# Rotary angles brought into range in radians, with sixteen VectorE operations for thirty

## The chip, the cores and the metric

The kernel runs on one core of one Trainium2 chip. The metric is device time in microseconds (us) of one execution; lower is better. A core has five engines that run side by side, each through its own queue in a fixed order: TensorE (PE; its weight loads are shown as PEld), VectorE (DVE), ScalarE (ACT), GpSimd (POOL) and SyncE (SP, which here only issues DMAs).

## What is computed

The reference is one layer of a hybrid block over 512 positions of 2048 channels: an RMS norm, one wide input projection, a retention branch (8 heads of 256) and a state-space branch, two branch projections merged by gates, an output projection, and a last norm. All of it is float32. The change touches only the rotation of q and k in the retention branch:

```python
def rope(t, positions):
    half = t.shape[-1] // 2
    inv_freq = ROPE_THETA ** (-jnp.arange(half, dtype=f32) / half)
    ang = positions.astype(f32)[..., None] * inv_freq
    cos, sin = jnp.cos(ang)[:, :, None, :], jnp.sin(ang)[:, :, None, :]
    t1, t2 = t[..., :half], t[..., half:]
    return jnp.concatenate([t1 * cos - t2 * sin, t2 * cos + t1 * sin], axis=-1)
```

Positions go up to about 100,000, so an angle can hold many whole turns. They have to be taken off before the sine is looked up, without losing the float32 product's own digits. The table of angles is 128 frequencies (partitions) by 512 positions, and is needed once: all heads share `sinR` and `cosR`.

## The kernel before, in words

Activations lie with channels on the partitions and the 512 positions along the free axis. Each projection is cut into units of 256 columns (`pair`, `unit`). A float32 operand is split into a high part in the matmul's own format (`whi`, by ScalarE, L152) and the rest (`wlo`, by VectorE, L155), and three products of parts stand for one float32 product (L242 to L244). A unit is either *plain* (four block products) or goes by seven block products for eight (`SEVEN`). The seven need sums of blocks: of the weights (VectorE, L259 to L265, from the buffer `wf` that SP loads at L256) and of the activations. The activations' operand tiles `a0` to `a7` (`first_half`) serve both kinds of unit; `b0` to `b7` (`second_half`) only the seven. `collected` brings a unit's result from the accumulator banks `pb` or `att` into a tile `o` (ScalarE L318 or L327, VectorE L319, L320 or L328 to L331). Only then can the next unit that uses the same banks begin.

The order of work: instructions are written down in program order, and a planner puts them in each engine's queue by priority, by dependences and by its own estimate of the time. Two things tie it down. `InOrder` (the lower-case `pe`, `act`, `dve`) keeps all instructions issued through one object in the order of their writing. `behind(ins, other)` keeps one instruction after another on the same engine. Operations written through either show line L122 in the profile.

The start (L427 to L488): SP loads the eight blocks of x; ScalarE squares them; TensorE sums the squares over the channels with a matrix of ones; VectorE adds the two halves of every second square beforehand (L456) and multiplies dt's weights by the norm weights (L461). Then come the norm's inverse root, the product for dt (L466), and for each block the normalization and `first_half` (L474 to L487). `formed` (L488) is the last ScalarE instruction of these, the cast of `a7`.

The rotary tables are a generator, `rotary_tables` (L386 to L424), that yields after each operation; `step(n)` runs the next n. Its operations use the tiles `Q`, `K` and one half of `S`, which are free at that time, and go through `dve`. One is issued at L446, and AHEAD[i] after block i (L459), 18 in all. Head 0 then computes the units of V and the gate together (`two_plain`, L597), writes the second halves in a loop with `step(4)` after each (L602 to L606), and `step(99)` issues what is left, the two sine activations on ScalarE among it. Next come the units Q (plain) and K (seven) of head 0, each followed by the rotation (L562 to L565), and then the scores. So the remaining rotary operations and the second halves form one ordered chain on VectorE.

The exponential of `a_log` (L497) is written for head 1, but its data are there early; it is bound `behind` `formed`.

Of the kernel before, what the change touches and what calls it, by code (L numbers as in the profile page):

```python
# [8 lines left out]
F32 = mybir.dt.float32  # L9
F32R = mybir.dt.float32r  # L10
I32 = mybir.dt.int32
AF = mybir.ActivationFunctionType
ALU = mybir.AluOpType
# [3 lines left out]
P = 128  # L17
# [16 lines left out]
C_ID, C_TRI, C_ONE, C_FREQ, C_END = 0, 128, 256, 384, 386  # L34


def _parts_of_inverse_two_pi():

    digits = 0.15915494309189533576888376337251436203445964574045644874766734405889
    from fractions import Fraction  # L40


    def atan_inv(n, bits):
        one = 1 << bits
        term = one // n
        total, k, sign = term, 1, 1
        while term:
            term //= n * n
            k += 2
            sign = -sign  # L50
            total += sign * (term // k)
        return total

    bits = 240
    pi = 4 * (4 * atan_inv(5, bits) - atan_inv(239, bits))
    inv = Fraction(1 << bits, 2 * pi)
    assert abs(float(inv) - digits) < 1e-15
    parts = []
    for i in range(5):
        step = Fraction(1, 1 << (14 + 12 * i))  # L60
        n = inv // step
        parts.append(float(n * step))
        inv -= n * step
    return parts


def constants():
# [37 lines left out]
PLAIN_Q, PLAIN_K = (0,), ()  # L105
PLAIN_B, PLAIN_X, PLAIN_Z, PLAIN_M = (), (), (), (15,)
PRIO = 30
AHEAD = (2, 1, 3, 1, 3, 1, 3, 3)
ROOT = 4
TERMS = ((0, 0), (0, 1), (1, 0))  # L110
BLOCK = (0, 4, 8, 7)
# [20 lines left out]
def hybrid_block(tc, A, out):  # L132
    nc = tc.nc
    PE, ACT, DVE, POOL, SP = nc.tensor, nc.scalar, nc.vector, nc.gpsimd, nc.sync
# [3 lines left out]
    cst = ctx.enter_context(tc.tile_pool(name="cst", bufs=1))  # L138
    hp = ctx.enter_context(tc.tile_pool(name="hp", bufs=1))
    wp = ctx.enter_context(tc.tile_pool(name="wp", bufs=1))  # L140
    op = ctx.enter_context(tc.tile_pool(name="op", bufs=2))
# [6 lines left out]
    def att_tile():  # L148
        return att.tile([P, T], F32, name="att")
# [9 lines left out]
    def behind(ins, other):  # L159

        tc.add_manual_dep(
            ins, other,
            mybir.DependencyInfo(mybir.DependencyClass.NoSync, mybir.DependencyReason.DATA),
            reason="order of issue")
# [135 lines left out]
    def two_plain(first, second):  # L300
        pts = banks(False), banks(True)
        steps = [product_steps(parts, pt, FOUR) for parts, pt in zip((first, second), pts)]
        for k in range(NP):
            for s in steps:
                next(s)
        return [collected(pt, True, False) for pt in pts]
# [34 lines left out]
    freq = cc[:, C_FREQ:C_FREQ + 1]  # L341
# [15 lines left out]

    eps = cst.tile([P, 1], F32, name="eps")
    POOL.memset(eps, EPS)

    def inverse_root(dst, ps, y, z, n, DVE=DVE, ACT=ACT):


        ACT.activation(y, ps, AF.Abs_reciprocal_sqrt, scale=1.0 / n, bias=eps)
        DVE.tensor_scalar(z, ps, -0.5 / n, -0.5 * EPS, op0=ALU.mult, op1=ALU.add)
        ACT.activation(dst, y, AF.Square)
        DVE.tensor_tensor(dst, dst, z, op=ALU.mult)
        DVE.scalar_tensor_tensor(dst, dst, 1.5, y, op0=ALU.add, op1=ALU.mult)
# [4 lines left out]
    def room(tag, dtype=F32):  # L373
        return bg.tile([P, 2, T], dtype, name=tag, tag=tag)
# [8 lines left out]
    cosR = rope.tile([P, T], F32, name="cosR")  # L383
    sinR = rope.tile([P, T], F32, name="sinR")

    def rotary_tables(x, fr, DVE):  # L386

        turn, a1, a2, ki = (x[i // 2][:, i % 2, :] for i in range(4))  # L390
        pos_i, ki = turn.bitcast(I32), ki.bitcast(I32)
        yield DVE.tensor_copy(fr, pos_i)
        yield DVE.tensor_scalar(fr, fr, freq, None, op0=ALU.mult)
        yield DVE.tensor_copy(a1.bitcast(F32R), fr)
        yield DVE.tensor_tensor(a2, fr, a1, op=ALU.subtract)
        c = _parts_of_inverse_two_pi()

        def wrap():
            yield DVE.tensor_copy(ki, turn)
            yield DVE.tensor_tensor(turn, turn, ki, op=ALU.subtract)  # L400

        first = True
        for a, cs in ((a1, c[:3]), (a2, c[:2])):
            for v in cs:
                dst = turn if first else fr
                yield DVE.tensor_scalar(ki, a, v, None, op0=ALU.mult)
                yield DVE.scalar_tensor_tensor(dst, a, v, ki, op0=ALU.mult, op1=ALU.subtract)
                if not first:
                    yield DVE.tensor_tensor(turn, turn, fr, op=ALU.add)
                if v == c[2]:  # L410
                    yield from wrap()
                first = False
        for a, cs in ((a1, c[3:]), (a2, c[2:4])):
            for v in cs:
                yield DVE.scalar_tensor_tensor(turn, a, v, turn, op0=ALU.mult, op1=ALU.add)
        yield from wrap()
        yield DVE.tensor_scalar(turn, turn, 0.49999997, -0.49999997, op0=ALU.min, op1=ALU.max)
        two_pi = 2.0 * math.pi
        ACT.activation(sinR, turn, AF.Sin, scale=two_pi)
        DVE.tensor_scalar(fr, turn, -1.0, None, op0=ALU.mult)  # L420
        DVE.tensor_tensor(fr, fr, turn, op=ALU.max)
        DVE.tensor_scalar(fr, fr, -1.0, 0.25, op0=ALU.mult, op1=ALU.add)
        ACT.activation(cosR, fr, AF.Sin, scale=two_pi)
        yield None  # L424


# [11 lines left out]
    steps = rotary_tables(angles, room("S")[:, 1, :], dve)  # L438

    def step(n):  # L440
        for _ in range(n):
            next(steps, None)
# [5 lines left out]
    for i in range(NP):  # L448
        x, y = raw[i], early[i][:, 2 * T:].rearrange("p (r t) -> p r t", r=2)
# [7 lines left out]
        for r in range(1 if i % 2 and i < NP - 1 else 2):  # L457
            pe.matmul(ps, ones, y[:, r, :], start=(i == r == 0), stop=(i == NP - 1 and r == 1))
        step(AHEAD[i])  # L459

# [13 lines left out]
    def normalized(i):  # L474
        for r in range(2):
            x, k = raw[i][:, r, :], 2 * i + r
            dve.scalar_tensor_tensor(x, x, nw[:, k:k + 1], R1, op0=ALU.mult, op1=ALU.mult)
        yield from first_half(i, dve, act)

    subs = []  # L480
    for i in range(NP):
        n = normalized(i)
# [5 lines left out]
    formed = act.last  # L488
# [59 lines left out]
    with tc.tile_pool(name="ret", bufs=1) as rp:  # L548
        for h in range(NH):
# [4 lines left out]
            c = h * DK  # L554

            def cols(o):
                return [w_in[:, o + c:o + c + DK]]
# [14 lines left out]
            def values(flat=None):  # L572
                hi = room("V", F32R if exact else F32).rearrange("p i (b e) -> p (i b) e", b=2)
                lo = room("Q", F32R).rearrange("p i (b e) -> p (i b) e", b=2) if exact else None
                if flat is None:
                    flat = pair(cols(VO), wide=h > 2)
                for i, x in enumerate((flat[:, 512:], flat[:, :512])):
                    ps, sl = att_tile(), slice(i * P, (i + 1) * P)
                    for tb in range(TB):
                        PE.transpose(ps[:, tb * P:(tb + 1) * P], x[:, tb * P:(tb + 1) * P], ident)  # L580
                    pv = ps.rearrange("p (b e) -> p b e", b=TB)
                    if exact:
                        split(hi[:, :, sl], lo[:, :, sl], pv)
                    else:
                        ACT.copy(hi[:, :, sl], pv)
                return hi, lo
# [9 lines left out]
            if h == 0:  # L596
                flats = two_plain(cols(VO), cols(GO))  # L597
                v, sg = values(flats[0]), gate(flats[1])
                gs = rp.tile([P, 2, 3, 256], F32, name="g", tag="g")
                ahead = [second_half(i, gs[:, i % 2], dve) for i in range(NP)]  # L600
                next(ahead[0])
                for i in range(NP):  # L602
                    if i + 1 < NP:
                        next(ahead[i + 1])
                    next(ahead[i])
                    step(4)  # L606
                step(99)
            q = rotate(QO, "Q")
            if exact:
# [13 lines left out]
            for sb in (3, 0, 1, 2):  # L623
                n, sl = T - sb * P, slice(sb * P, (sb + 1) * P)
# [8 lines left out]
                t = near if sb == 2 else wide[:, BLOCK[sb] * P:][:, :n]  # L633
# [10 lines left out]
            if h:  # L644
                v = values()
# [5 lines left out]
            for lb in range(TB):  # L651
                ps = att_tile()
                for sb in range(lb + 1):
                    terms = TERMS if exact else ((0, 0),)
                    for m, (a, b) in enumerate(terms):
# [9 lines left out]
                                         op0=ALU.mult, op1=ALU.mult)  # L665
# [13 lines left out]
    with tc.tile_pool(name="ssd", bufs=1) as sp:  # L679
# [29 lines left out]
        for g in range(NG):  # L709
# [14 lines left out]
            for jj in range(2):  # L724
# [5 lines left out]
                for e in range(2):  # L730
# [9 lines left out]
                    for c in range(TB):  # L740
# [6 lines left out]
                                       op=ALU.mult)  # L747
# [6 lines left out]
                    for c in range(1, TB - 1):  # L754
                        for i in range(2):
# [3 lines left out]
                                                     op0=ALU.mult, op1=ALU.add)  # L759
                    pi = att_tile()  # L760
# [4 lines left out]
                    for i in range(2):  # L765
                        for c in range(TB):
                            ACT.activation(L[:, i, c, :], L[:, i, c, :], AF.Relu, scale=-1.0,  # L767
                                           bias=At[:, c, h0 + i:h0 + i + 1])
# [29 lines left out]
    with tc.tile_pool(name="br", bufs=1) as bp:  # L798
# [23 lines left out]
        for i in range(NP):  # L822
            x, t = branch(w_r, i), ptile(gr_d, i)
# [8 lines left out]
        for i in range(NP):  # L832
            s, m = scaled(i), ptile(m_d, i)
            x = branch(w_s[:D, :], i)
# [4 lines left out]
        for i in range(NP):  # L839
            if i == NP - 1:  # L840
                last = raw_tile(i)
            x = branch(w_s[D:, :], i)
            s, q = ptile(s2_d, i), ptile(ps_d, i)
# [12 lines left out]
    with tc.tile_pool(name="fin", bufs=1) as fp:  # L856
# [4 lines left out]
        for i in range(NP - 1):  # L861
            if i == 1:
                second_halves([xo[n].rearrange("p r (h t) -> p (r h) t", h=2)[:, 0:3, :] for n in (6, 7)])
            t = xo[i]
# [12 lines left out]
        t = xo[NP - 1]  # L877
# [85 lines left out]
```

## Time and profile before

| | |
|---|---|
| time, median of 3 runs | 2705.46 us (2701.65 to 2706.98) |
| the profiled execution | 2705.3 us, of which the span of the profile is 2703.4 |
| TensorE, weight loads | busy 2660.9 us (98%), 2562.7 us (95%) |
| VectorE | busy 2455.0 us (91%) |
| ScalarE, GpSimd | busy 1365.0 us (50%), 198.1 us (7%) |
| DMA | 370.88 MB, mean 137 GB/s |
| granted clock of TensorE | 0.998 |

A row of the profile names an engine, a line of the kernel, the operation, the tile written and the tiles read, the shape, and durations. In a row of the order of time the first number is the start in us, the second the duration; the bracket gives the idle time of the engine before it and what ended that. In a row of the waits the numbers are the total in us, the count, and the longest. Matmuls are pipelined and their ends are modelled, so a busy TensorE isn't TensorE at its peak.

### The profile page before, as it was taken

Reading aid. Unit: us, or ns where it says so; the run is one execution under the profiler, and the core shown is the slowest. Engines: PE = TensorE matmul, PEld = TensorE weight load, DVE = VectorE, ACT = ScalarE, POOL = GpSimd, SP = SyncE. Lnnn points to the kernel's source line nnn. Section 1 sums busy time; section 2 is a strip of 40 time slices with the busy share of each in tenths; the row PEclk is TensorE's granted clock in tenths of the full one; section 3 lists DMA queues with packets and bytes.
Section 4 is the critical chain, followed back from the end, with each engine's and each line's share of the span. In section 5 each row is a group of like instructions: output and inputs, shape, how many; then the busy total and the mean of one; then the engine's idle time right before and its main releaser. Section 6 shows DMA issues by size and latency. Waiting matters only on the chain.

```text
span 2703.4 us, 52528 instructions
## 1 busy us (share of the span) xinstructions
PE 2660.9 (98%) x20792; PEld 2562.7 (95%) x20792; DVE 2455.0 (91%) x3912; ACT 1365.0 (50%) x1920; POOL 198.1 (7%) x122
## 2 busy tenths in 40 slices
PE   8999999999999999999999999999999999999998
PEld 5899999999999999999999999999999989899897
DVE  7998989888989999999999999999989899998897
ACT  4534444444446655555565555556564443433543
POOL 0010000000000100010101000010100001100211
PEclk9999999999999999999999999999999999999999
DMA  5332333333343434343444434344464656757434
GB/s 162 92 109 88 102 105 102 107 104 100 106 119 108 139 124 131 113 131 121 132 139 127 136 113 130 124 129 132 131 233 138 204 193 196 241 167 233 162 125 141
DMA packets 332855, 370.88 MB, mean 137 GB/s; under 512 B 24384, under 2 KB 297024, under 8 KB 332608
## 3 DMA queue, kind: packets, MB, share of 16 engines
q1 hardware_dynamic: 317744, 329.77, 39.4%
q10 hardware_dynamic: 14864, 37.75, 3.8%
q8 instruction: 163, 2.67, 0.4%
q14 instruction: 84, 0.69, 0.1%
HBM read 325.76 MB, written 41.68 MB: 136 GB/s over the span
## 4 chain that ended last, share of the span: by engine, by line
PE 80%; DVE 9%; DMA 5%; issue 2%; ACT 2%; SPq 1%; POOL 0%; DVEq 0%; ACTq 0%; POOLq 0%
PE pb L244 21%; PE pb L242 20%; PE pb L243 20%; DVE wlo L155 3%; PE att L244 3%; PE att L243 3%; PE att L242 3%; DMA wf<-in_w_in_dram 2%; PE pb L240 2%; DMA L<-A_d 2%; PE att L656 1%; PE att L774 1%; PE att L122 1%; DVE wf L259 1%; PE pb L122 1%
## 5 line engine op out<-in xcount | busy, mean ns | idle before, releaser
L152 ACT CAST whi<-wf 128x896 fp32r<-128x896 f32 (+1 forms) x968 | 828.7, 904 | 690.3 <-DVE wf L265 376.4
L155 DVE TENSOR_TENSOR wlo<-wf,whi 128x896 fp32r<-128x896 f32 (+1 forms) x968 | 1017.9, 1066 | 77.2 <-ACT whi L152 48.0
L244 PE MATMUL pb<-a,wlo 128*128 128x256 f32 (+1 forms) x3296 | 928.5, 293 | 4.5 <-DVE wlo L155 4.1
L242 PE MATMUL pb<-a,whi 128*128 128x256 f32 (+1 forms) x3040 | 875.7, 293 | 6.2 <-DVE o L328 1.9
L243 PE MATMUL pb<-a,whi 128*128 128x256 f32 (+1 forms) x3040 | 875.0, 292 | 0.0
L243 PE MATMUL pb<-b,whi 128*128 128x256 f32 x2304 | 652.8, 283 | 0.8 <-DVE b L122 0.7
L242 PE MATMUL pb<-b,whi 128*128 128x256 f32 x2304 | 651.7, 283 | 0.0
L244 PE MATMUL pb<-b,wlo 128*128 128x256 f32 x2304 | 647.0, 283 | 0.0
L244 PEld LDWEIGHTS pb<-a,wlo 128*128 128x128 f32 x3296 | 613.4, 191 | 19.9 <-DVE wlo L155 9.9
L242 PEld LDWEIGHTS pb<-a,whi 128*128 128x128 f32 x3040 | 579.9, 191 | 25.4 <-issue 4.3
L243 PEld LDWEIGHTS pb<-a,whi 128*128 128x128 f32 x3040 | 580.0, 191 | 12.8
L243 PEld LDWEIGHTS pb<-b,whi 128*128 128x128 f32 x2304 | 440.0, 191 | 1.2 <-DVE b L122 1.2
L242 PEld LDWEIGHTS pb<-b,whi 128*128 128x128 f32 x2304 | 439.9, 191 | 0.0
L244 PEld LDWEIGHTS pb<-b,wlo 128*128 128x128 f32 x2304 | 437.7, 191 | 0.0
L259 DVE TENSOR_TENSOR wf<-wf 128x512 f32<-128x512 f32 x432 | 306.0, 708 | 45.2 <-DMA wf<-in_w_in_dram 23.8
L265 DVE TENSOR_TENSOR wf<-wf 128x256 f32<-128x256 f32 x432 | 194.2, 450 | 1.6
L264 DVE TENSOR_TENSOR wf<-wf 128x256 f32<-128x256 f32 x432 | 189.4, 438 | 0.3
L244 PE MATMUL att<-a,wlo 128*128 128x256 f32 (+1 forms) x512 | 155.3, 311 | 2.8 <-DVE wlo L155 2.8
L767 ACT ACTIVATE L<-L,sst 128x128 f32<-128x128 f32 x256 | 78.5, 389 | 113.9 <-DMA L<-A_d 104.7
L243 PE MATMUL att<-a,whi 128*128 128x256 f32 (+1 forms) x416 | 130.7, 316 | 0.0
L242 PE MATMUL att<-a,whi 128*128 128x256 f32 (+1 forms) x416 | 128.1, 316 | 0.0
L244 PEld LDWEIGHTS att<-a,wlo 128*128 128x128 f32 x512 | 95.5, 189 | 10.0 <-DVE wlo L155 4.4
(253 smaller groups left out, 3059.9 us busy)
## 6 DMA issues: line engine op xcount, KB each, us to landing
wf<-in_w_in_dram SPq DMA_DIRECT2D x640, 256.0 KB, 3.1
wf<-in_w_br_ssd_dram SPq DMA_DIRECT2D x128, 256.0 KB, 3.6
wf<-in_w_out_dram SPq DMA_DIRECT2D x72, 256.0 KB, 3.0
wf<-in_w_in_dram SPq DMA_DIRECT2D x128, 128.0 KB, 2.7
L<-A_d SPq DMA_DIRECT2D x32, 512.0 KB, 4.8
wf<-in_w_br_ret_dram SPq DMA_DIRECT2D x64, 256.0 KB, 3.1
ys_d<-Q ACTq DMA_DIRECT2D x32, 256.0 KB, 3.5
r<-ys_d SPq DMA_DIRECT2D x16, 512.0 KB, 7.2
```

Source lines behind the costliest of these rows:

```text
L122: ins = getattr(self.engine, name)(*args, **kw).ins
L152: high = ACT.copy(dst_hi, src).ins
L155: return DVE.tensor_tensor(dst_lo, src, dst_hi.bitcast(F32), op=ALU.subtract).ins
L240: PE.matmul(pt[0], wh, both(k, x), start=b not in started, stop=(k == NP - 1), skip_group_check=True)
L242: PE.matmul(o, wh, xh, start=b not in started, stop=False, skip_group_check=True)
L243: PE.matmul(o, wh, xl, start=False, stop=False, skip_group_check=True)
L244: PE.matmul(o, wl, xh, start=False, stop=(k == NP - 1), skip_group_check=True)
L259: first = DVE.tensor_tensor(f2[:, :, 4:6, :], f2[:, :, 1:3, :], f2[:, :, 0:1, :].to_broadcast([P, 2, 2, P]), op=ALU.subtract)
L264: DVE.tensor_tensor(f2[:, :, 0, :], f2[:, :, 2, :], f2[:, :, 4, :], op=ALU.add)
L265: DVE.tensor_tensor(f2[:, :, 6, :], f2[:, :, 3, :], f2[:, :, 0, :], op=ALU.subtract)
L656: PE.matmul(ps[:, :DK], block(BLOCK[sb] + lb - sb, *pt[a]), v[b][:, sb, :], start=(sb == 0 and m == 0), stop=(sb == lb and m == len(terms) ...
L767: ACT.activation(L[:, i, c, :], L[:, i, c, :], AF.Relu, scale=-1.0, bias=At[:, c, h0 + i:h0 + i + 1])
```

## The change

The old form split the angle into two parts, multiplied them by three to five short parts of 1/(2 pi), dropped the whole turns product by product and kept the sum as a fraction of a turn: thirty VectorE operations. The new one stays in radians. It finds how often 16384 turns go into the angle (`many`), and subtracts that many times 16384 x 2 pi in four short parts; it finds how many single turns are left (`few`), subtracts these in three short parts, and then takes one more round for the last turn. That is sixteen operations, fifteen of them issued by AHEAD after the first, so none is left for the loop over second halves; its `step(4)` goes. The cosine is the sine of a quarter turn minus the absolute angle, with the minus and the quarter now in the activation itself (`scale`, `bias`), the quarter in a tile that GpSimd fills. The two sines are bound behind `formed`. The parts come from a helper, `_parts`, on the host.

```diff
-AHEAD = (2, 1, 3, 1, 3, 1, 3, 3)
+AHEAD = (2, 1, 3, 1, 2, 1, 2, 3)
...
+    quarter = cst.tile([P, 1], F32, name="quarter")
+    POOL.memset(quarter, 0.5 * math.pi)
...
-        turn, a1, a2, ki = (x[i // 2][:, i % 2, :] for i in range(4))
-        pos_i, ki = turn.bitcast(I32), ki.bitcast(I32)
-        yield DVE.tensor_copy(fr, pos_i)
-        yield DVE.tensor_scalar(fr, fr, freq, None, op0=ALU.mult)
-        yield DVE.tensor_copy(a1.bitcast(F32R), fr)
-        yield DVE.tensor_tensor(a2, fr, a1, op=ALU.subtract)
...
-        for a, cs in ((a1, c[:3]), (a2, c[:2])):
-            for v in cs:
-                dst = turn if first else fr
-                yield DVE.tensor_scalar(ki, a, v, None, op0=ALU.mult)
-                yield DVE.scalar_tensor_tensor(dst, a, v, ki, op0=ALU.mult, op1=ALU.subtract)
-                if not first:
-                    yield DVE.tensor_tensor(turn, turn, fr, op=ALU.add)
-                if v == c[2]:
-                    yield from wrap()
-                first = False
-        for a, cs in ((a1, c[3:]), (a2, c[2:4])):
-            for v in cs:
-                yield DVE.scalar_tensor_tensor(turn, a, v, turn, op0=ALU.mult, op1=ALU.add)
-        yield from wrap()
-        yield DVE.tensor_scalar(turn, turn, 0.49999997, -0.49999997, op0=ALU.min, op1=ALU.max)
-        two_pi = 2.0 * math.pi
-        ACT.activation(sinR, turn, AF.Sin, scale=two_pi)
-        DVE.tensor_scalar(fr, turn, -1.0, None, op0=ALU.mult)
-        DVE.tensor_tensor(fr, fr, turn, op=ALU.max)
-        DVE.tensor_scalar(fr, fr, -1.0, 0.25, op0=ALU.mult, op1=ALU.add)
-        ACT.activation(cosR, fr, AF.Sin, scale=two_pi)
+        pos, r, many, few = (x[i // 2][:, i % 2, :] for i in range(4))
+        pos, many, few = (t.bitcast(I32) for t in (pos, many, few))
+        big = _parts(TURNS * _two_pi(), (8, -1, -10))
+        small = _parts(_two_pi(), (-6, -15))
+
+        def less(dst, n, part):
+            return DVE.scalar_tensor_tensor(dst, n, -part, r, op0=ALU.mult, op1=ALU.add)
+
+        def whole(n, a, scale):
+            return DVE.tensor_scalar(n, a, scale, None, op0=ALU.mult)
+
+        turns = 0.5 / math.pi
+        yield DVE.tensor_copy(fr, pos)
+        yield DVE.tensor_scalar(r, fr, freq, None, op0=ALU.mult)
+        yield whole(many, r, turns / TURNS)
+        yield less(r, many, big[0])
+        yield less(r, many, big[1])
+        yield less(fr, many, big[2] + big[3])
+        yield whole(few, fr, turns)
+        yield less(r, few, small[0])
+        yield less(r, many, big[2])
+        yield less(r, few, small[1])
+        yield less(r, many, big[3])
+        yield less(r, few, small[2])
+        yield whole(few, r, turns)
+        yield less(r, few, 2.0 * math.pi)
+        yield DVE.tensor_scalar(r, r, 3.1415925, -3.1415925, op0=ALU.min, op1=ALU.max)
+        yield DVE.scalar_tensor_tensor(fr, r, -1.0, r, op0=ALU.mult, op1=ALU.max)
+        behind(ACT.activation(sinR, r, AF.Sin).ins, formed)
+        behind(ACT.activation(cosR, fr, AF.Sin, scale=-1.0, bias=quarter).ins, formed)
...
                     next(ahead[i])
-                    step(4)
                 step(99)
```

More of the change, by code (lines that the diff above doesn't have):

```diff
@@ L34, with _two_pi @@
 C_ID, C_TRI, C_ONE, C_FREQ, C_END = 0, 128, 256, 384, 386
-def _parts_of_inverse_two_pi():
-    digits = 0.15915494309189533576888376337251436203445964574045644874766734405889
+def _two_pi():
     from fractions import Fraction
@@ L54, in _parts_of_inverse_two_pi, with _parts @@
     bits = 240
-    pi = 4 * (4 * atan_inv(5, bits) - atan_inv(239, bits))
-    inv = Fraction(1 << bits, 2 * pi)
-    assert abs(float(inv) - digits) < 1e-15
+    return Fraction(8 * (4 * atan_inv(5, bits) - atan_inv(239, bits)), 1 << bits)
+TURNS = 1 << 14
+def _parts(value, steps):
+    from fractions import Fraction
     parts = []
[L59 to L64, printed above, removed]
+    for step in steps:
+        q = round(value / Fraction(2) ** step) * Fraction(2) ** step
+        parts.append(float(q))
+        value -= q
+    return parts + [float(np.float32(float(value)))]
 def constants():
@@ L386, in rotary_tables @@
     def rotary_tables(x, fr, DVE):
-        turn, a1, a2, ki = (x[i // 2][:, i % 2, :] for i in range(4))
-        pos_i, ki = turn.bitcast(I32), ki.bitcast(I32)
-        yield DVE.tensor_copy(fr, pos_i)
-        yield DVE.tensor_scalar(fr, fr, freq, None, op0=ALU.mult)
-        yield DVE.tensor_copy(a1.bitcast(F32R), fr)
-        yield DVE.tensor_tensor(a2, fr, a1, op=ALU.subtract)
[L396 to L400, printed above, removed]
@@ L402, in rotary_tables @@
-        first = True
-        for a, cs in ((a1, c[:3]), (a2, c[:2])):
-            for v in cs:
-                dst = turn if first else fr
-                yield DVE.tensor_scalar(ki, a, v, None, op0=ALU.mult)
-                yield DVE.scalar_tensor_tensor(dst, a, v, ki, op0=ALU.mult, op1=ALU.subtract)
-                if not first:
-                    yield DVE.tensor_tensor(turn, turn, fr, op=ALU.add)
-                if v == c[2]:
-                    yield from wrap()
-                first = False
```

## The prediction

> **What bounds the kernel now.** I read the page first, then busy time by stretches, then the waits of TensorE's weight loads, then VectorE's instructions in order of time.
>
> ```profile
> span 2703.4 us, 52528 instructions
> PE 2660.9 (98%) x20792; PEld 2562.7 (95%) x20792; DVE 2455.0 (91%) x3912; ACT 1365.0 (50%) x1920; POOL 198.1 (7%) x122
> PE 80%; DVE 9%; DMA 5%; issue 2%; ACT 2%; SPq 1%; POOL 0%; DVEq 0%; ACTq 0%; POOLq 0%
> ```
>
> Busy time and the chain by engine: TensorE sets the time. An operation on VectorE is worth something only where TensorE waits for VectorE. The rotary angles are computed once, so at most two places matter: the first 22 us, and the rest of head 0. The answer by stretches of that rest (length, then PE, PEld, DVE, ACT, POOL busy):
>
> ```profile
> 66.00:97.00 31.00, 30.23 (x138) 24.79 (x136) 29.48 (x54) 17.77 (x26) 0.00 (x0) 1.00 0.36 115
> 97.00:140.00 43.00, 39.80 (x317) 38.52 (x318) 42.14 (x65) 17.63 (x23) 0.00 (x0) 1.00 0.30 89
> 140.00:200.00 60.00, 57.69 (x436) 54.98 (x435) 55.02 (x97) 23.07 (x30) 7.32 (x4) 1.00 0.35 109
> ```
>
> From 66 to 140 us VectorE is busy 71.6 of 74 us, and TensorE is not: it lacks 0.77 + 3.20 = 3.97 us. The busy time of a matmul includes a modelled tail, so the waits of the weight loads, which start it, say more. From 66 to 125 us they are:
>
> ```profile
> PEld pb L242 <- DVE o L319: 1.9, 1, 1.9
> PEld pb L243 <- DVE b L122: 1.2, 2, 0.9
> PEld pb L244 <- DVE wlo L155: 1.2, 2, 0.9
> PEld pb L242 <- ACT o L327: 1.0, 1, 1.0
> PEld pb L242 <- DVE o L328: 0.4, 1, 0.4
> ```
>
> Five groups, 5.7 us together, and four of them name VectorE. The fifth, a copy on ScalarE, lies in the same stretch. So TensorE stands still there for 4.0 us (by its busy time) to 5.7 us (by its weight loads) because VectorE is late. What makes it late:
>
> ```profile
> 69.56 0.68 DVE L122 SCALAR_TENSOR_TENSOR S<-K 128x512 f32<-128x512 f32 x1
> ...
> 93.41 0.42 DVE L122 TENSOR_SCALAR S<-S 128x512 f32<-128x512 f32 x1
> ...
> 96.02 0.95 DVE L122 TENSOR_TENSOR b<-g,b 128x768 fp32r<-128x768 f32 x1
> ...
> 97.23 0.42 DVE L319 TENSOR_TENSOR o<-pb,o 128x256 f32<-128x256 f32 x1
> ...
> 119.42 0.95 DVE L122 TENSOR_TENSOR b<-g,b 128x768 fp32r<-128x768 f32 x1
> ```
>
> The first two rows are the first and the last of twelve rotary operations, from 69.56 to 93.41 us, shuffled among the splits of weights (wlo) and the second halves of the operands (g, b). The addition at 97.23, for which K's product of head 0 waits 1.9 us, stands behind a b. The eighth and last b ends at 120.37; K's remaining products need it.
>
> **The change, part by part.** *The late operations.* Of the old thirty, eighteen are issued during the first 20 us (one, then AHEAD's 17), and twelve in the loop over second halves. All sixteen new ones are issued early (one plus 15), so VectorE does nothing for the angles after that. The price of the twelve, by groups from 66 to 124 us (count, busy, mean ns):
>
> ```profile
> L122 DVE SCALAR_TENSOR_TENSOR Q<-Q 128x512 f32<-128x512 f32 x2 | 1.4, 686 | 0.0
> ...
> L122 DVE TENSOR_TENSOR Q<-Q,K 128x512 f32<-128x512 f32 x1 | 0.7, 686 | 0.0
> ...
> L122 DVE TENSOR_SCALAR S<-S 128x512 f32<-128x512 f32 x1 | 0.4, 421 | 0.0
> ...
> L122 DVE CAST K<-Q 128x512 int32<-128x512 f32 x1 | 0.4, 417 | 0.0
> ```
>
> Eight have two tensor inputs (5 scalar_tensor_tensor, 3 tensor_tensor), four have one (3 tensor_scalar, 1 cast): 8 x 0.686 + 4 x 0.42 = 7.2 us. VectorE's idle time from 66 to 140 us is only 2.4 us, so that much work comes out of a nearly full queue: more than the 5.7 us that TensorE waits. The bound therefore passes back to TensorE, and not all 7.2 us can be gained. I take the five waits one by one. The addition at L319 loses the queue ahead of it: 1.9 becomes 0.3, which is what an end of a product costs where VectorE is on time (the row for L328 has 0.4 for one). The second halves end some 7 us earlier, well before they are needed: 1.2 becomes 0. The two late wlo: 1.2 becomes 0.3, since near the end of a product a split can still be the last to come. The ScalarE copy at L327, which I put down to its queue waiting for VectorE's sums of weights: 1.0 becomes 0.3. The addition at L328 stays at 0.3. Left over 1.2, gained 4.5 us. The ends: 1.9 (only the first wait goes) and 5.7 (all go).
>
> *The start.* Here the eighteen become sixteen, but each new one uses the result of the one before. The rows from 9.5 us on, to see what a dependent operation costs:
>
> ```profile
> 9.52 0.69 DVE L122 TENSOR_TENSOR e<-e 128x512 f32<-128x512 f32 x1 [1.38 <-ACT e L122]
> 10.12 0.68 DVE L122 TENSOR_TENSOR K<-S,Q 128x512 f32<-128x512 f32 x1
> ...
> 11.18 0.69 DVE L122 SCALAR_TENSOR_TENSOR Q<-Q,K 128x512 f32<-128x512 f32 x1
> 11.91 0.43 DVE L122 TENSOR_SCALAR K<-Q 128x512 int32<-128x512 f32 x1
> 12.25 0.68 DVE L122 TENSOR_TENSOR e<-e 128x512 f32<-128x512 f32 x1
> 12.85 0.69 DVE L122 SCALAR_TENSOR_TENSOR S<-Q,K 128x512 f32<-128x512 f32 x1
> 13.57 0.69 DVE L122 TENSOR_TENSOR Q<-Q,S 128x512 f32<-128x512 f32 x1
> ...
> 19.89 1.22 DVE L122 TENSOR_TENSOR e<-e,nw 128x1024 f32<-128x1024 f32 x1
> ...
> 20.85 0.19 PEld L122 LDWEIGHTS att<-e,cc 128*128 128x128 f32 x1 [0.24 <-issue]
> 21.80 0.20 PEld L122 LDWEIGHTS att<-r,e 128*64 128x64 f32 x4 [0.76 <-DVE e L122]
> ```
>
> From a two-input operation to one that needs its result: 11.91 - 11.18 = 0.73 and 13.57 - 12.85 = 0.72 us. To one that doesn't: 10.12 - 9.52 = 0.60. A short one: 12.25 - 11.91 = 0.34; I take 0.46 with a dependence, adding the same 0.12. Three new operations come before 9.52, thirteen after it: ten long, three short, and two more sums of squares between them. From 10.12: 10 x 0.72 + 3 x 0.46 + 2 x 0.60 = 9.8 us, so the product with the norm weights (19.89) begins at 19.9, where it is. That is the term that decides, since TensorE's first product with dt's weights waits 0.76 for it, against 0.24 between the loads before. I take 0, with ends of 0.5 gained (0.76 - 0.24, were the spacing 0.60 throughout) and 0.2 lost (0.02 more for each of the ten).
>
> *The sines.* Both inputs will lie ready at 20 us, so the planner may place the sines wherever ScalarE is free; the new `behind(..., formed)` keeps them after the last cast of head 0's first halves. The exponential of a_log has the same bond, and went right there:
>
> ```profile
> 64.33 1.28 ACT L497 ACT_TABLE_LOAD   x1
> 65.63 0.26 ACT L497 ACTIVATE na<-na 128x64 f32<-128x64 f32 x1
> 67.26 0.84 ACT L200 CAST b<-g 128x768 fp32r<-128x768 f32 x1 [1.38 <-DVE g L122]
> ...
> 75.46 0.84 ACT L200 CAST b<-g 128x768 fp32r<-128x768 f32 x1 [2.12 <-DVE g L122]
> ...
> 86.12 1.28 ACT L419 ACT_TABLE_LOAD   x1
> 87.41 0.63 ACT L419 ACTIVATE sinR<-Q 128x512 f32<-128x512 f32 x1
> ...
> 95.26 1.28 ACT L593 ACT_TABLE_LOAD   x1
> ```
>
> I expect table load, sine, cosine in front of or behind it: 1.28 + 2 x 0.63 = 2.5 us more at 64 us, and as much less at 86 to 95; three table loads as now. ScalarE idles 1.38 us before 67.26 and 2.12 before 75.46, which covers it but for 1.2 us on the casts between; their readers on VectorE are late anyway. Cost taken: 0. Uncovered, it is 1.2, which is inside the end of 1.9 gained. The added fill of one column on GpSimd lies in an idle queue.
>
> Here the Trainium skill is less kind to a moved sine ("ScalarE: Activation LUTs", What ACT_TABLE_LOAD costs): it puts a switch at a load of about 1.28 us and a drain of about 1.38. The trace shows the load and no drain: 64.33 + 1.28 = 65.61, and the activation starts at 65.63. By the page the gain would be estimated at up to 1.4 us less, 3.1.
>
> *Sum.* The profiled execution took 2705.3 us (span 2703.4 and 1.9 around it): 2705.3 - 4.5 - 0 + 0 = 2700.8. The median, 2705.46, lies 0.2 above it: 2701.0. A measurement of this kernel can tell about 0.2% from no change, 5.4 us, so this is a gain just short of what counts as faster.
>
> **The rivals.**
>
> ```profile
> PEld att L629 <- DVE K L155: 1.5, 1, 1.5
> PEld att L629 <- ACT S L152: 1.3, 1, 1.3
> ...
> PEld pb L244 <- DVE wlo L155: 2.0, 2, 1.9
> ```
>
> These are waits of the weight loads from 125 to 400 us. *More is gained:* VectorE arrives at head 1 ahead, and the splits for its scores, for which TensorE waits 1.5 + 1.3 us, come in time as well. For: VectorE is busy 55.0 of 60 us there. Against: they are a chain, rotation, split, product, that starts when K's product ends. 2701.0 - 2.8 = 2698.2, and with the leftover 1.2 and the 0.5 of the start 2696.5.
>
> *Little is gained:* the dependences and not the queue hold VectorE. wf has three buffers and the splits must wait for TensorE to release theirs, so the freed 7.2 us turn into idle time on VectorE. Then only the first wait, 1.9 less 0.3, goes: 2703.9. Against: VectorE hardly idles from 97 to 140.
>
> *Slower:* the planner orders the queues by its own estimates, and a shorter angle chain moves every later place. One split that lands behind a collected product costs 1.9 us, as the row for wlo shows for one. If such a wait recurred in each of the seven later heads, 13.3 - 4.5 = 8.8 us would be lost: 2714. It decides from the third recurrence (5.7 against 4.5). Against: those heads' dependences are untouched, and the trace has only one such wait up to 400 us.
>
> *It doesn't do what it says:* the sixteen might not all be placed early. Issue order fixes them on VectorE, ahead of the norm product, so I give this nothing of its own.
>
> **How the numbers follow.** Forecast 0.48 (2699 to 2702.5), more gained 0.26 (2694 to 2698.5), little gained 0.18 (2703 to 2706), slower 0.08 (2707 to 2714). Range: 2695.5 leaves out less than a tenth below, 2706.0 the slower case above. Faster by over 5.4 us, below 2700.05: nearly all of the second case and a quarter of the first, 0.38. Slower, above 2710.9: most of the last case, 0.06. Between: 0.56.
>
> **What would show it.** No VectorE operation on the angles after 22 us; ten of the sixteen at about 0.69 us; dt's first product within 0.2 us of 21.80; both sines and a table load between 64 and 69 us; the last b before 115 us; K's first matmul within 0.4 us of Q's last; the waits from 66 to 125 us down from 5.7 to about 1.2; and everything after that some 4.5 us earlier to the end. I am wrong if that stretch keeps its waits, if the start moves by over 0.5 us, or if waits after 200 us add up to a different sum.

## The result, and the profile after

The changed kernel took 2694.92 us, the median of 11 runs (2689.1 to 2702.51), against 2705.4 us (2699.4 to 2706.98) for the kernel before in the same comparisons. The ratio is 0.997, with a 95% interval of 0.9961 to 0.9979: 8.1 us faster, between 5.7 and 10.6 (the ratio is not that of the two medians, which stand 10.5 us apart). The median lies 0.6 us below the range of the prediction; the ratio on the median known then gives 2697.3, inside it.

The page of the changed kernel: span, busy time, and the chain by engine.

```profile
span 2692.8 us, 52521 instructions
PE 2657.0 (99%) x20792; PEld 2561.7 (95%) x20792; DVE 2447.4 (91%) x3898; ACT 1365.3 (51%) x1920; POOL 198.3 (7%) x123
...
PE 83%; DVE 8%; DMA 4%; issue 2%; ACT 2%; POOL 1%; SPq 0%; DVEq 0%; ACTq 0%; POOLq 0%
```

VectorE has 7.6 us less to do (2455.0 - 2447.4), its share of the chain has fallen from 9 to 8%, and TensorE's has risen from 80 to 83%. The same three stretches as before (length, then PE, PEld, DVE, ACT, POOL busy):

```profile
66.00:97.00 31.00, 31.00 (x147) 25.95 (x146) 30.46 (x55) 22.97 (x34) 0.00 (x0) 1.00 0.36 111
97.00:140.00 43.00, 43.00 (x339) 41.36 (x338) 40.15 (x65) 14.34 (x18) 0.55 (x1) 1.00 0.35 105
140.00:200.00 60.00, 60.00 (x482) 59.28 (x481) 54.52 (x92) 25.03 (x33) 5.04 (x3) 1.00 0.33 102
```

TensorE is busy all the 134 us; before, it lacked 6.3. The waits of the weight loads from 66 to 125 us, 5.7 us before, are gone: that answer has no rows left. From 125 to 200 us, where 2.8 us stood at L629, one row is left, four short steps that were there before too:

```profile
PEld att L631 <- issue: 1.0, 4, 0.2
```

VectorE in order of time: the last angle operation, the product with the norm weights behind it, and much later the addition for which K's product had waited, with the last b.

```profile
19.37 0.69 DVE L124 SCALAR_TENSOR_TENSOR S<-Q 128x512 f32<-128x512 f32 x1
...
19.98 1.22 DVE L124 TENSOR_TENSOR e<-e,nw 128x1024 f32<-128x1024 f32 x1
...
94.77 0.44 DVE L321 TENSOR_TENSOR o<-pb,o 128x256 f32<-128x256 f32 x1
...
95.10 0.97 DVE L124 TENSOR_TENSOR b<-g,b 128x768 fp32r<-128x768 f32 x1
```

The last b ends at 96 us instead of 120. ScalarE's part, in the same view:

```profile
63.80 1.28 ACT L422 ACT_TABLE_LOAD   x1
65.09 0.63 ACT L422 ACTIVATE sinR<-Q 128x512 f32<-128x512 f32 x1
65.63 0.71 ACT L423 ACTIVATE cosR<-S,quarter 128x512 f32<-128x512 f32 x1
66.36 1.28 ACT L497 ACT_TABLE_LOAD   x1
67.66 0.26 ACT L497 ACTIVATE na<-na 128x64 f32<-128x64 f32 x1
...
78.50 1.28 ACT L593 ACT_TABLE_LOAD   x1 [1.58 <-DVE o L322]
```

The sines stand in front of the exponential, three loads as before. To place the gain I use two marks in each trace: the start of dt's product on TensorE, and the DMA that stores head 3's result (the fourth such store). Marks within one trace are free of the start of the run and of what the rest of it does. The store of head 3, before and after:

```profile
443.55 0.37 ACTq L671 DMA_DIRECT2D yr_d<-S  x1
```

```profile
434.52 0.37 ACTq L670 DMA_DIRECT2D yr_d<-S  x1
```

dt's product starts at 21.80 before and 21.54 after, so the way is 421.8 us before and 413.0 after: 8.8 us shorter, all of what the ratio shows. (The two spans differ by 10.6; the rest is mostly the part after head 3, which differs by 5.8 us between the kernel before and e9 below, though TensorE's queue is the same in both there; so nothing is read from it.)

### The profile page after: what moved, and what is told of

It is laid out like the page before. It is cut to its first block, busy times and chain, and to the rows that moved or that the text cites. A ratio compares the mean times of both kernels' runs of the same rounds, so it can differ in the third digit from the quotient of the medians.

```text
span 2692.8 us, 52521 instructions
## 1 busy us (share of the span) xinstructions
PE 2657.0 (99%) x20792; PEld 2561.7 (95%) x20792; DVE 2447.4 (91%) x3898; ACT 1365.3 (51%) x1920; POOL 198.3 (7%) x123
## 4 chain that ended last, share of the span: by engine, by line
PE 83%; DVE 8%; DMA 4%; issue 2%; ACT 2%; POOL 1%; SPq 0%; DVEq 0%; ACTq 0%; POOLq 0%
PE pb L246 22%; PE pb L244 21%; PE pb L245 21%; PE att L246 3%; DVE wlo L157 3%; PE att L245 3%; PE att L244 3%; PE pb L242 2%; DMA L<-A_d 1%; DMA wf<-in_w_in_dram 1%; PE att L655 1%; PE att L773 1%; PE att L124 1%; PE pb L124 1%; PE att L628 1%
```

## The experiments

All were run beside the kernel before on one chip each. That kernel took 2699 to 2701 us there, so ratios are compared, and the way between the two marks. A second profile of the changed kernel shows how steady the way is (e7: 412.8).

| kernel | way, us | weight-load waits 66 to 125 us | 125 to 200 us (without issue) | ratio, interval |
|---|---|---|---|---|
| before | 421.8 | 5.7 | 2.8 | 1 |
| changed | 413.0 | 0 | 0 | 0.997, 0.9961 to 0.9979 |
| e1 twelve fills | 416.1 | 3.6 | 0 | 0.9986, 0.9976 to 0.9995 |
| e2 six fills | 412.0 | 0.3 | 0 | 0.9962, 0.9947 to 0.9977 |
| e3 twenty-four fills | 426.3 | 10.1 | 1.2 | 1.0026, 1.0015 to 1.0038 |
| e4 late sines | 414.3 | 1.5 | 0 | 0.9972, 0.9963 to 0.9981 |
| e5 twelve fills, sines at their old place | 416.7 | 4.0 | 0 | 0.9981, 0.9972 to 0.999 |
| e6 old thirty, moved | 416.3 | 0.6 | 0 | 0.9979, 0.997 to 0.9987 |
| e7 changed again | 412.8 | 0 | 0 | 0.997, 0.9959 to 0.9981 |
| e8 no turns subtracted | 413.0 | 0 | 0 | 0.9958, 0.9946 to 0.997 |
| e9 new operations, late | 421.8 | 4.3 | 2.8 | 1.0002, 0.9994 to 1.0011 |
| e10 twelve fills, sines last | 421.2 | 3.3 | 4.4 | 0.9998, 0.9989 to 1.0008 |
| e11 twelve fills in head 3 | (fills lie inside) | 0 | 0 | 0.9982, 0.9973 to 0.999 |
| e12 sines not bound | 412.3 | 0 | 0 | 0.9977, 0.9967 to 0.9987 |

### Filling VectorE's queue again: e1, e2, e3

```diff
                     next(ahead[i])
+                    for kind in {0: "llll", 1: "llsl", 2: "ssls"}.get(i, ""):
+                        m, f = angles[1][:, 0, :], angles[1][:, 1, :]
+                        if kind == "l":
+                            dve.scalar_tensor_tensor(f, m, 0.0, f, op0=ALU.mult, op1=ALU.add)
+                        else:
+                            dve.tensor_scalar(f, f, 1.0, None, op0=ALU.mult)
                 step(99)
```

This is e1; e2 has `{0: "llll", 1: "ll"}`, and e3 each string twice.

> The changed kernel, with twelve operations (eight scalar_tensor_tensor, four tensor_scalar, 128x512, on a tile that nothing else uses there) put back in the places of the old late twelve; their values are used by nothing, and the sines stay early. Theory of the full queue (VectorE's freed 7.2 us between 66 and 140 us are what TensorE gained): all of it comes back, weight-load waits of about 5.7 us from 66 to 125 us and 2.8 us from 125 to 200 us, time within 2 us of the kernel before, 2705. Rival, the place of the sines and of the tile S (table load at 64 instead of 86 us, the gate's tile free earlier): the fill costs next to nothing, time about 2695 to 2697. Rival, a lucky order of the planner: no fixed sum, anything from 2690 to 2710, and the waits elsewhere.

> As the run with twelve, but six long operations only (4.1 us of VectorE), behind the first two second halves. Full queue: VectorE idles 3.4 us between 66 and 140 us after the change, so the first 3.4 us cost nothing or little and the rest shows: 1 to 3 us over the changed kernel, 2696 to 2698. If every microsecond counted, without slack, 4 us: 2699. Place of the sines: 2695. Planner's luck: no order by dose.

> As the run with twelve, but twenty-four operations (14.3 us of VectorE). Full queue: beyond the twelve each further microsecond is one that TensorE waits, 7 us over the run with twelve, about 2711 to 2713. Place of the sines: as the changed kernel, 2695 to 2698. Planner's luck: no order by dose.

The order by dose is there beyond the slack: 3.1 us for twelve, 13.3 for twenty-four, and nothing (even 0.9 us less) for six, whose 4.1 us nearly fit in the 3.4 that VectorE idles. But e1 missed my number: the twelve bring back 3.1 of 8.8 us by the way, and by the ratio about half (0.0016 of 0.0030). Its waits from 66 to 125 us:

```profile
PEld pb L245 <- DVE b L124: 1.4, 2, 1.1
PEld pb L244 <- DVE o L321: 1.0, 1, 1.0
PEld pb L244 <- ACT o L329: 0.7, 1, 0.7
PEld pb L244 <- DVE o L330: 0.5, 1, 0.5
```

The kinds are those of before, with 3.6 us instead of 5.7, and from 125 to 200 us nothing came back. So the work on VectorE is a cause, and not the only one. The doses are not clean, though: with each of them the planner changed TensorE's order too. Compared place by place in the traces (by line and tiles), another matmul than in the changed kernel stands at 985, 1497 and 708 of the 20792 places in e1, e2 and e3, while e4, e7, e8 and e12 have the changed kernel's order throughout. In e3 something is added. By stretches of 5 us:

```profile
105.00:110.00 5.00, 1.70 (x12) 1.28 (x11) 5.00 (x9) 3.04 (x4) 0.00 (x0) 1.00 0.22 77
110.00:115.00 5.00, 2.45 (x9) 1.45 (x7) 5.00 (x10) 0.90 (x2) 0.00 (x0) 0.63 0.35 105
115.00:120.00 5.00, 2.22 (x10) 2.22 (x11) 4.86 (x9) 1.89 (x3) 0.00 (x0) 0.50 0.01 3
120.00:125.00 5.00, 5.00 (x38) 5.00 (x37) 5.00 (x9) 2.30 (x3) 0.00 (x0) 0.85 0.35 105
```

VectorE is full, TensorE mostly idle, and the granted clock (third from the end) falls to 0.63 and 0.50 behind the idle time. That may be one reason why the second twelve cost 10.2 us, more than their 7.2 us of work; no run separates it.

### The sines' place: e4, e5, e12

```diff
-                ahead = [second_half(i, gs[:, i % 2], dve) for i in range(NP)]
+                casts = InOrder(tc, ACT)
+                ahead = [second_half(i, gs[:, i % 2], dve, casts) for i in range(NP)]
...
-                step(99)
+                    if i == 5:
+                        kept, formed = formed, casts.last
+                        step(99)
+                        formed = kept
```

This is e4. e5 has the twelve fills of e1 as well and `i == 2`; e12 is the changed kernel without the two `behind`.

> The changed kernel with only the two sines moved back: bound behind the cast of b6, so at about 88 to 92 us, table load with them; no VectorE operation is added. Full queue: VectorE's work is unchanged, the sines are needed at 101 us, so within 1 us of the changed kernel, 2694 to 2697. Place of the sines: the gain goes, 2702 to 2705, as the gate's Silu waits for the cosine's tile again.

> The changed kernel with the twelve filling operations and, beside them, the two sines back behind the cast of b3 (their old place, about 86 us). The twelve alone left 3.6 us of weight-load waits from 66 to 125 us, against 5.7 of the kernel before, and none from 125 to 200, against 2.8. If the old sines' place was the other part, it shows only together with a full VectorE queue: about the kernel before, ratio 0.999 to 1.001, the 2.8 us back. If not, the ratio stays at that of the twelve alone, 0.9986, and the rest of the gain is the planner's order, with head 0's scores at 136 us as there.

> The changed kernel without the bond of the sines behind formed; the planner then puts table load, sine and cosine at about 20 us, ahead of the inverse root, which needs its own table again: 1.28 + 1.2 + 1.28 = 3.8 us in ScalarE's queue. The norm's root is about 2.3 us late, against some 2 us of room (a0's cast ends at 27.5 us, the first product starts at 29.5): 0 to 1 us over the changed kernel. Rival, the start is a chain through ScalarE: 2 to 3.8 us over it, ratio 0.998.

The sines alone cost 1.3 us by the way when they are late (two waits of TensorE for additions on VectorE, 1.0 and 0.5 us), and nothing that the ratio can tell. Added to the twelve, at their old place, they cost 0.6 us: the expectation that the two together would be the kernel before fell. Not bound at all, they run at 18 to 21 us with a table load before and one after:

```profile
17.94 1.28 ACT L422 ACT_TABLE_LOAD   x1
19.24 0.63 ACT L422 ACTIVATE sinR<-Q 128x512 f32<-128x512 f32 x1
19.92 0.72 ACT L423 ACTIVATE cosR<-S,quarter 128x512 f32<-128x512 f32 x1
20.55 0.60 ACT L154 CAST whi<-wf 128x512 fp32r<-128x512 f32 x1
21.17 1.28 ACT L124 ACT_TABLE_LOAD   x1
22.46 0.69 ACT L124 ACTIVATE e<-att,eps 128x512 f32<-128x512 f32 x1
```

The root starts at 22.46 instead of 21.64 and the way is 412.3 us: the change's bond behind `formed` gains nothing that these runs can tell. The interval of e12's ratio reaches from 0.9967 to 0.9987 and overlaps that of the changed kernel.

### Number or place: e6, e9

e6 is the kernel before, with its thirty operations:

```diff
         next(n)
+        if i < 6:
+            step(2)
     formed = act.last
...
-                    step(4)
                 step(99)
```

The last three VectorE operations of the generator yield as well, and the sines follow them, bound behind `formed`. e9 is the changed kernel with `AHEAD = (1, 0, 1, 0, 1, 0, 0, 0)` and `step(4)` in the loop again: the new arithmetic in the old places.

> The kernel before with its old thirty operations, only moved: the late twelve stand two by two behind the first six of the first halves (30 to 60 us, where VectorE idles 2.4 us at every second one), and the sines behind the cast of a7 as in the change. Full queue: the count doesn't matter, the place does, so the gain comes whole: ratio 0.997, waits of 66 to 125 us near 0, provided that the operands a1 to a6 are not late by it. Rival, fewer operations: VectorE's work is that of the kernel before, 7.2 us more than the change, so little gain, ratio 0.999 to 1.

> The changed kernel with the new arithmetic kept but its operations in the old places: four of the sixteen early, twelve in the loop over second halves, the sines after them. The planner makes TensorE's queue of the kernel before of it, with head 1's first scores 977 matmuls in, against 993 in the changed one and 999 with the twelve filling operations. Full queue together with the planner's order: the gain goes whole, from dt's first product to the store of head 3 421.8 us as before (413.0 in the changed kernel, 416.1 with the filling), the waits of L629 from 125 to 200 us are back (2.8 us), ratio 0.999 to 1.001. Rival, the new arithmetic itself is faster wherever it stands: ratio 0.997 to 0.998.

e9 took the gain away whole: ratio 1.0002, way 421.8, the very number of before. The loop holds twelve operations here as in the kernel before, and the fourteen fewer all come off the start: the new arithmetic as such is worth nothing, and what counts is what stands in the loop. (Six operations there, in e2, cost nothing.) Its waits from 125 to 200 us, with those of the kernel before to the tenth:

```profile
PEld att L629 <- DVE K L157: 1.5, 1, 1.5
PEld att L629 <- ACT S L154: 1.3, 1, 1.3
PEld att L632 <- issue: 1.0, 4, 0.2
```

e6 is the counterpart. Its waits from 66 to 125 us are 0.6, those of L629 are gone, and still it keeps only 5.5 of the 8.8 us. What is missing lies where I put the twelve (waits up to 66 us):

```profile
PEld pb L242 <- ACT a L122: 3.7, 4, 1.3
```

Four of the first halves came late by them. 416.3 - 3.7 is 412.6, about the changed kernel's way: if this wait is taken off, the old thirty gain in the emptied stretch what the new sixteen do. Only this one place was tried for the old twelve; that the smaller number is what lets all of them go early is argued from it, not shown.

### The planner's order: e10

e10 is e5 with `i == 6`, so the sines wait for the cast of b7.

> The changed kernel with the twelve filling operations and with the sines bound behind the cast of b7, so that the planner sees the rotation late; head 1's first scores come 984 matmuls in, head 0's later products in pieces as in the kernel before. If the second part of the gain is the planner's order, set off by late tables over a full VectorE queue: from dt's first product to the store of head 3 419 to 423 us, ratio about 1. If it needs the real operations: 416 to 417, ratio 0.998.

It came out at 421.2 and ratio 0.9998: the kernel before again, from filling operations that compute nothing. What e9, e10 and the kernel before have in common shows in TensorE's queue, which is fixed before the run. In these three (before, e9, e10), head 1's first scores start at 186.0, 186.4 and 185.5 us, and the last transposes of head 0's retention (L668 of before) behind them, at 187.3, 187.7 and 186.3. In all the other kernels the transposes come first, 12 to 16 us ahead of head 1's scores (166.4 against 181.9 us in the changed kernel). Only these three have the waits for head 1's split of K, in e10 from 125 to 200 us:

```profile
PEld att L638 <- DVE K L157: 1.8, 1, 1.8
PEld pb L246 <- DVE wlo L157: 1.3, 2, 1.1
PEld att L638 <- ACT S L154: 1.3, 1, 1.3
```

The traces show how the order brings these waits. The split of head 1's K writes the tile `S`, of which there is only one, and head 0's result stays in `S` until its store has landed; the store needs the last transposes. The last operation of the rotation of K, the store of head 0 and the split, before and after:

```profile
181.89 0.69 DVE L565 TENSOR_TENSOR o<-o,K 128x512 f32<-128x512 f32 x1
...
189.50 0.38 ACTq L671 DMA_DIRECT2D yr_d<-S  x1
...
192.73 0.83 ACT L152 CAST S<-o 128x768 fp32r<-128x768 f32 x1
```

```profile
170.51 0.38 ACTq L670 DMA_DIRECT2D yr_d<-S  x1
...
177.62 0.68 DVE L565 TENSOR_TENSOR o<-o,K 128x512 f32<-128x512 f32 x1
...
178.38 0.83 ACT L154 CAST S<-o 128x768 fp32r<-128x768 f32 x1 [1.02 <-issue]
```

Before, the rotation is done at 182.6 us, but the split starts at 192.73: 0.4 us after the store has landed (189.50 + 2.8), with two casts of weights just in front of it in ScalarE's queue. In e9 and e10 it starts 3.2 and 3.4 us after the store as well. After the change the store is long over, and the split follows the rotation within 0.1 us.

So the second part of the gain goes with a change of TensorE's order. Work on VectorE alone doesn't undo it (e1, e3), late sines alone don't (e4), and both with the sines at about 86 us don't (e5); the full queue with the sines behind it does (e9, e10). An order alone, with VectorE's queue free, wasn't tried, and why the planner's estimate tips there stays open.

### The start: e8

```diff
-        yield whole(many, r, turns / TURNS)
-        yield less(r, many, big[0])
...
-        yield less(r, few, 2.0 * math.pi)
```

> The changed kernel without its reduction: it leaves out the twelve operations that find and subtract whole turns, so that its sines are those of clipped angles; four operations are left of sixteen. This prices what the start still pays for the angles. My term for the start was that VectorE's chain ends at 19.9 us and costs TensorE 0.76 - 0.24 = 0.5 us before dt's product: 0.5 us less than the changed kernel, no more, since TensorE's sums of squares end when they do. Rival, the chain holds up the whole start (the halves of the squares stand behind it): 1 to 3 us less.

(`AHEAD` becomes `(1, 0, 0, 0, 0, 0, 0, 2)` with it.) The way is 413.0, exactly that of the changed kernel. dt's product can be compared as well: TensorE's first square of x starts at 7.67, dt's product at 21.70, 14.0 us later, against 13.5 after and 14.1 before. VectorE is busy 1.9 of the 6 us from 10 to 16 us, instead of 5.8, and its product with the norm weights now ends at 20.23; still the start isn't shorter, and the gap in front of dt's product is the same 0.76 us:

```profile
21.70 0.20 PEld L124 LDWEIGHTS att<-r,e 128*64 128x64 f32 x4 [0.76 <-issue]
```

So this gap was no wait for VectorE; the last section shows what differs in the start. The ratio, 0.9958, lies lower than that of the changed kernel, but the intervals overlap, and no mark in the trace supports a gain.

### The same work elsewhere: e11

```diff
+            if h == 3:
+                for kind in "llllllslssls":
+                    if kind == "l":
+                        dve.scalar_tensor_tensor(sinR, cosR, 0.0, sinR, op0=ALU.mult, op1=ALU.add)
+                    else:
+                        dve.tensor_scalar(sinR, sinR, 1.0, None, op0=ALU.mult)
             k = rotate(KO, "K")
```

> The changed kernel with twelve operations of the same size put into head 3 instead, between its two rotations (they multiply the sine table by one and add zero to it). Full queue: what counts is whether VectorE has room where they stand. From 200 to 700 us it is busy 449 of 500 us, so 7.2 us find room within one head of some 89 us: 0 to 2 us over the changed kernel, ratio 0.997 to 0.998. Rival, a VectorE operation costs its time anywhere: 7 us, ratio 0.9997.

Neither number was right: the ratio is 0.9982, some 3 us over the changed kernel (the intervals overlap by 0.0006). The store of the last head says 4.2 us: it comes 771.6 us after dt's product, against 767.5. From 200 to 400 us the waits rise from 2.0 to 6.5 us:

```profile
PEld pb L246 <- DVE wlo L157: 1.9, 2, 1.7
PEld att L634 <- DVE K L157: 1.8, 1, 1.8
PEld att L637 <- DVE o L565: 1.5, 1, 1.5
PEld att L634 <- ACT S L154: 0.9, 1, 0.9
PEld pb L242 <- ACT whi L154: 0.4, 1, 0.4
```

Free time on VectorE in the mean (51 us of 500) didn't take up 7.2 us, because the operations stood in front of the rotation and the split of K, for which TensorE waits: head 3's rotation of K starts at 364.58 us instead of 355.70. TensorE's order is another one here too, from its 2354th matmul on, so this run is not free of the planner either.

## Why the prediction was right, and where it was not

The direction and the mechanism held: VectorE's full queue held TensorE up, and the twelve late operations were part of it (e1, e3, and e6 from the other side). The sum was too small: 4.5 us, against 8.1 by the ratio (5.7 to 10.6) and 8.8 by the way. What came is the rival *more is gained*, and the time lies in the range because the range had been drawn for that rival too. Point by point:

- *The late operations.* Priced at 7.2 us; VectorE's whole busy time fell by 7.6; right.
- *The five waits.* Sized 4.5, measured 5.7: all five went, where I had left 0.3 at each end of a product and 0.3 for late splits. With VectorE ahead these ends cost nothing here.
- *The start.* Sized 0, with ends of 0.5 and -0.2; e8 gives 0. But my reason for the lower end, that dt's product waits 0.76 us for the norm product, was a misreading: in e8 the norm product ends 1.5 us ahead of it, and the gap is the same 0.76.
- *The sines.* They went where I said, at 63.80 with three loads, and their cost is nil. The Trainium skill's page "ScalarE: Activation LUTs" (What ACT_TABLE_LOAD costs) would add a drain of about 1.38 us to each switch; the changed kernel's rows again show none that holds up the next activation (63.80 + 1.28 = 65.08, next start 65.09), and the gain was not the 3.1 us estimated by it but more than 4.5.
- *The step that failed* is the one that left head 1 out: "Against: they are a chain, rotation, split, product, that starts when K's product ends." The chain was not the bound: in the kernel before the split starts 10 us after the rotation has ended (192.73 against 182.6), because its tile `S` still holds head 0's result until the store at 189.50 has landed. e1 has the twelve operations in VectorE's queue and yet none of those waits, while e9 and e10 have them, and with them head 0's late transposes. This case, "more is gained", was given 0.26, and 2696.5 for all of it; it is the one that came.
- *Faster by over 0.2%* was given 0.38, and 0.3% was measured.

No kernel here is clearly better than the changed one. e2, with six useless operations, has a way that is 0.9 us shorter and a ratio of 0.9962; its interval contains 0.997, and its TensorE order is another one again. Whether that 0.9 us is the order's wasn't tried.

## What to carry to other kernels

Price an edit on an engine that isn't the bound by the stretch where it stands: count what that engine idles there, and what waits for it. Clearing the angles out of head 0 went with 8.8 us; the new arithmetic with as many operations in the old place was worth nothing, and taking twelve operations out of the start was worth nothing either. Where a planner sets the order of the queues, part of a gain can be a new order on the engine that is the bound; compare the queues' orders before telling a gain by the work removed, look for the buffer that the new order frees earlier (here `S`), and refill the freed place with useless work to see how much of it was that work.

## What the runs showed of the hardware

The first matmuls of the program start 0.85 us apart and later ones 0.43, for the same form, although the granted clock is 1.00 in every stretch of 2 us from 10 to 16 us. Weight loads in the changed kernel:

```profile
10.76 0.33 PEld L124 LDWEIGHTS att<-e,cc 128*128 128x128 f32 x1 [0.52 <-DVE e L124]
11.61 0.33 PEld L124 LDWEIGHTS att<-e,cc 128*128 128x128 f32 x1 [0.52 <-issue]
12.43 0.19 PEld L124 LDWEIGHTS att<-e,cc 128*128 128x128 f32 x1 [0.49 <-issue]
12.86 0.19 PEld L124 LDWEIGHTS att<-e,cc 128*128 128x128 f32 x1 [0.24 <-issue]
```

The step came 4.4 us after the first load here, and in the kernel before 5.9 us after it (13.55 against 7.68). Half of those 1.5 us is about the difference in the start, 14.1 against 13.5 us; in e8, with few operations on VectorE, it was 14.0, with the step 5.8 us after the first load, so the angles don't set it. And in e3 the granted clock was 0.63 and then 0.50 in the two stretches of 5 us behind one in which TensorE was busy for 1.70 us. What this cost beyond the wait itself wasn't measured.
